# The Differential layer rebuilt: weights split one layer ahead, the convolution on VectorE alone and its inputs placed among the attention heads

## The chip, the cores and the metric

The kernel runs on one NeuronCore of a Trainium2 chip. The metric is the device time of one execution in microseconds (us); the median of three runs of the kernel before is 2931.03 us (2930.87 to 2932.01). Engines are named as in the profile: PE is TensorE (matmul), PEld its weight loads, DVE VectorE, ACT ScalarE, POOL GpSimd, SP the engine that issues the DMAs.

## The reference

Four mixer layers in a row (stages a0, b, c, a1), then two layers that each have a mixer and a SwiGLU feed-forward (m0, f0, m1, f1), on 512 tokens of width 1024 in float32. The change touches m0, the Differential layer, above all:

```python
def sandwich(x, g_pre, g_post, fn):
    return x + rmsnorm(fn(rmsnorm(x, g_pre)), g_post)

def even_mixer(t, ...):                     # m0
    proj = t @ w_in
    y_a = diff_attention(proj[..., :3 * DIFF_WIDTH], ...)
    y_b = conformer_conv(proj[..., 3 * DIFF_WIDTH:], dw_w, dw_b, ln_g, ln_b)
    return jnp.concatenate([y_a, y_b], axis=-1) @ w_out

def diff_attention(qkv, ...):               # 4 heads, two score maps each
    ...
        p = jax.nn.softmax(jnp.where(chunk_causal_mask(i, s), sc, -jnp.inf), axis=-1)
        w = p[:, :, 0] - lam * p[:, :, 1]
        return jnp.einsum('bhqk,bkhe->bqhe', w.astype(v.dtype), v)
    ...
    o = rmsnorm(o, subln) * (1.0 - lam_init)

def conformer_conv(g, dw_w, dw_b, ln_g, ln_b):   # 512 channels, 31 taps
    u = g[..., :CONV_CHANNELS] * jax.nn.sigmoid(g[..., CONV_CHANNELS:])
    y = lax.conv_general_dilated(u, dw_w[:, None, :], ..., feature_group_count=CONV_CHANNELS) + dw_b
    return jax.nn.silu(layernorm(y, ln_g, ln_b))
```

m1, the other mixer, is a state-space layer beside a latent attention; f0 and f1 are `(silu(h @ w_gate) * (h @ w_up)) @ w_down`.

## The kernel before

The activations x stay transposed on the chip: eight blocks of 128 features by 512 tokens. A float32 product is made of three matmuls in a reduced float32 form (fp32r). Every weight chunk of 128 x 1024 (512 KB) is loaded by SP into `wr`, copied by ACT into a high part `wh`, and the low part is `wl = wr - wh`, a subtraction on DVE; then the products wh·xh, wl·xh and wh·xl go into one PSUM sum. This is `wchunk`; `wr`, `wh` and `wl` have three buffers each. One chunk feeds 24 matmuls of 512 columns. `gemm_T` makes one output block from one chunk, `gemm_tok` a block of tokens from four.

In m0 every third chunk is split on POOL instead (`share`), in two halves (L284), and so are two of the four chunks with which the next layer begins (`wchunk(srcs[1], D, G)` in `sandwich_end`). m0 first makes all four convolution inputs (eight chunks `m0_wab`), then queries and keys of heads 0 and 1 (`project(0)`), the values, and `project(1)`. Of the 31 taps of a channel block 23 run on DVE as one multiply-add each (tile `cv`), 8 on ACT and POOL (L1091, L1092, tile `cvg`). Convolution and heads are generators in the list `tasks`; `tick` moves each of them on by one step between the matmuls of the other work. When all four convolution outputs are ready, `sandwich_end` multiplies by `m0_wo`, whose rows are ordered convolution first and heads 0 to 3 behind it, normalizes, adds to x, splits the new x (`xh`, `xl`) and starts the next layer's first panels by halves of the tokens.

A scheduler fixes each engine's order of instructions when the program is built, so every engine, and SP's DMA queue too, works through a list: an instruction that waits holds up what stands behind it. Nearly all DVE and PE instructions carry line L205, that of a helper, so they are told apart by their tiles: `g` and `a` are PSUM tiles, `x` the activations, `y` the inputs of an output product, `P` and `Ps` softmax rows, `mxc` a row maximum.

Of the kernel before, what the change touches and what calls it, by code (L numbers as in the profile page):

```python
# [4 lines left out]
P = 128  # L5
NT = 512
# [34 lines left out]
def prepare(inp):  # L41
# [75 lines left out]
    A["m0_wo"] = _panels(np.concatenate([w[512:], w[:512]], axis=0))  # L117
# [62 lines left out]
def build(nc, tc, A, out, stages=("a0", "b", "c", "a1", "m0", "f0", "m1", "f1")):  # L180
# [40 lines left out]
    with ctx:  # L221
# [49 lines left out]
        share = [0, 0]  # L271

        def wchunk(src, n, eng=None):
            if eng is None:
                share[1] += 1
                eng = G if share[0] and share[1] % share[0] == 0 else V
            wr = early.pop(0) if early else fetch(src, n)
# [550 lines left out]
        def layer_c(nxt):  # L828
            with ExitStack() as c:
                pp = newpool(c, "pcl")  # L830
                pp5 = newpool(c, "pcm", 5)
                X = state["X"]
                first, sc, sb = opening([A["c_wx"][i] for i in range(3)], X)
                csc = load(pp, "c_sc")
                ic = load(pp, "c_ic")
                pads = [tl(pp, (P, 16 + NT), f"pad{i}") for i in range(6)]
                for t in pads:
                    V.memset(t[:, 0:16], 0.0)
                npad = [0]

                def pad():
                    npad[0] += 1
                    return pads[npad[0] % 6]
                new_norm(nxt)
                for half in range(2):
                    Y = []
                    for g in (2 * half, 2 * half + 1):
                        wd = 2 << g
                        M = []
                        for i in range(4):  # L850
                            ps = first.pop(0) if first else gemm_T(A["c_wx"][g * 4 + i], X)
# [12 lines left out]
                            V.tensor_tensor(df[:, :16], fx, xc[:, 16:32], op=SUB)  # L864
                            M.append(split(pp5, "m", df))
                        Z = []
                        for i in range(4):
                            pz = gemm_T(A["c_wz"][g * 4 + i], X)
                            z = tl(pp, (P, NT), "z", bufs=5)
                            V.tensor_tensor(z, pz, sb, op=MUL)  # L870
                            S.activation(z, z, AF.Silu)
                            Z.append(z)
                        for i in range(4):
                            ps = gemm_T(A["c_wg"][g, i], M)
                            V.scalar_tensor_tensor(Z[i], ps, csc[:, g * 4 + i:g * 4 + i + 1], Z[i],
                                                   op0=MUL, op1=MUL)
                            Y.append(split(py, "y", Z[i]))
                    for m in range(KD):
                        ps = gemm_T(A["c_wo"][half, m], Y)
                        V.tensor_tensor(xs[m], xs[m], ps, op=ADD)  # L880
                        if half:
                            finish_x(m)()

        def ffn_first(l):
            return [A[f"f{l}_w{n}"][i] for i in range(2) for n in "gu"] if f"f{l}" in stages else None

        def m1_first():
            return [A["m1_win"][i] for i in (2, 0, 1, 3)] if "m1" in stages else None


        def sandwich_end(W, Y, O, fresh, grow, srcs, pre=None, k0=0):
# [82 lines left out]
            if srcs:  # L974
                W1 = wchunk(srcs[1], D, G)
# [13 lines left out]
            W2 = wchunk(srcs[2], D, G)  # L989
# [55 lines left out]
        def layer_m0(nxt):  # L1045
            with ExitStack() as c:
# [3 lines left out]
                first, sc, sb = opening([A["m0_wab"][i] for i in range(3)], X)  # L1050
# [23 lines left out]
                def conv(i, up, y):  # L1074
                    def w(k):
                        return dw[:, i * 31 + k:i * 31 + k + 1]

                    def u(k):
                        return up[:, 2 + k:2 + k + NT]
                    nv = 31 - CONV_G  # L1080
                    g = tl(pm, (P, NT), "cvg")
                    for k in range(nv):
                        if k == 0:
                            V.tensor_scalar(y, u(0), w(0), cb[:, i:i + 1], op0=MUL, op1=ADD)
                            S.activation(g, u(nv), AF.Copy, scale=w(nv))
                        else:
                            V.scalar_tensor_tensor(y, u(k), w(k), y, op0=MUL, op1=ADD)
                        q = nv + 1 + k // 3
                        if k % 3 == 2 and q < 31:
                            t = tmp()  # L1090
                            S.activation(t, u(q), AF.Copy, scale=w(q))  # L1091
                            G.tensor_tensor(g, g, t, op=ADD)  # L1092
                        if k % 4 == 4 - 1:
                            yield
                    V.tensor_tensor(y, y, g, op=ADD)

                def convs():
                    for i in range(4):
                        yield from conv(*CV[i])
                        if i == 1:  # L1100
                            total = tl(pm, (P, NT), "cb")
                        if i:
                            G.tensor_tensor(total, C[0] if i == 1 else total, C[i], op=ADD)
                    ps = psum_a()
                    PE.matmul(ps, lhsT=ones, rhs=total, start=True, stop=True)
# [3 lines left out]
                    ln = SumSq(4)  # L1109
                    for i in range(4):  # L1110
                        V.tensor_tensor(C[i], C[i], mu, op=SUB)
                        ln.add(C[i], i)
                    yield
                    r = small(4, "lnr")
                    rstd(r, ln.sums(), 1.0 / 512, 1e-5)
                    lb = bcast(diagonal(r), pm, "cb")
                    yield
                    for i in range(4):
# [5 lines left out]
                        Y[i] = split(py, "y", C[i], 0.5)  # L1124
                        yield
                CV = []
                for i in range(4):
                    pu = first.pop(0) if first else gemm_T(A["m0_wab"][2 * i], X)
                    pb = first.pop(0) if first else gemm_T(A["m0_wab"][2 * i + 1], X)
# [10 lines left out]
                    if i == 0:  # L1140
                        tasks.append(convs())


                def project(a):

                    pss = gemm_tok([A["m0_wqk"][a, i] for i in range(4)], X, NT, 2)
# [27 lines left out]
                def attend(h, T):  # L1174
# [40 lines left out]
                    Y[4 + h] = split(py, "y", ps, sub)  # L1215
                share[:] = [3, 0]
                q = project(0)
                T = [flip_qk(q, 0), flip_qk(q, 1)]
                pss = gemm_tok([A["m0_wv"][i] for i in range(4)], X, NT, 2)
# [4 lines left out]
                tasks.append(attend(1, T[1]))  # L1224
                q = project(1)
# [6 lines left out]
                sandwich_end(A["m0_wo"], Y, [tl(pa, (P, NT), "qkT") for _ in range(KD)], True, 8, ffn_first(0), k0=4)  # L1232


# [132 lines left out]
        def layer_m1(nxt):  # L1367
            with ExitStack() as c:
# [91 lines left out]
                def glu():  # L1460
# [4 lines left out]
                    wh, wl = wchunk(A["s_wg"], 512)  # L1465
# [27 lines left out]
                for i in range(2):  # L1493
                    ps = gemm_T(A["m1_win"][4 + i], X)
# [7 lines left out]
                wh, wl = wchunk(A["m1_wk"], 768)  # L1502
# [10 lines left out]
                wh, wl = wchunk(A["m1_wv"], 768)  # L1513
# [11 lines left out]
                for a in range(3):  # L1525
                    wh, wl = wchunk(A["m1_wq"][a], 1024)
# [53 lines left out]
                sandwich_end(A["m1_wo"], Y, O + [tl(pm, (P, NT), f"u{i}") for i in range(2)], True, 10, ffn_first(1))  # L1580


        def layer_f(l, nxt):
            with ExitStack() as c:
# [31 lines left out]
        pdr0 = newpool(ctx, "pdr0", space=bass.MemoryType.DRAM)  # L1616
# [42 lines left out]
```

## Time and profile before

| | |
|---|---|
| median of 3 runs | 2931.03 us |
| profiled execution, its own time | 2936.18 us |
| its span | 2933.7 us |
| mean granted TensorE clock | 0.976 |
| busy: PE, DVE, ACT, POOL | 96%, 56%, 36%, 12% |
| bytes moved | 270 MB, mean 92 GB/s |

The span is from the first to the last instruction; the execution's own time lies 2.5 us above it. In the trace m0 is at about 1643 to 1958 us, f0 at 1958 to 2250, m1 at 2250 to 2570, layer c at 973 to 1277. In a window row each engine has its busy time in that stretch and its instructions in brackets; PEclk is the granted clock as a share of full speed.

### The profile page before, as it was taken

The numbers are of one execution on the slowest core, as the hardware profiler recorded it, in microseconds if no ns is written. First come the engines' busy times: TensorE is split into PE (matmuls) and PEld (weight loads), VectorE is DVE, ScalarE is ACT, GpSimd is POOL, SyncE is SP. The second block draws the span as 40 slices with busy tenths as digits, with TensorE's granted clock in tenths as the row PEclk, the third lists the DMA queues.
The fourth block names the chain that finished last, engine by engine and source line by source line (L and its number), as shares of the span: only waits on it lengthen the run. The fifth ranks groups of instructions, "written<-read, shape, count | busy, mean of one in ns | idle before, by whom it ended". The sixth has DMA issues, their size and how long they took to land. (4 is left out here: it accounts for less than half of the span.)

```text
span 2933.7 us, 34524 instructions
## 1 busy us (share of the span) xinstructions
PE 2820.6 (96%) x13488; PEld 2331.9 (79%) x13488; DVE 1642.2 (56%) x3023; ACT 1051.9 (36%) x1679; POOL 347.3 (12%) x272
## 2 busy tenths in 40 slices
PE   8999999999999999999999987889999979999998
PEld 7888888888888888888888865678888845888886
DVE  4454654545556554544445697896443696543434
ACT  4322344444444322333223445442222435432222
POOL 2000000000000111210010252120000341300001
PEclk9999999999999999999999997889999999999999
DMA  4222332222223232322222211123332320132222
GB/s 161 94 86 94 129 111 87 87 80 94 72 94 95 94 101 89 120 93 94 93 94 92 90 63 44 48 96 136 111 105 92 113 90 22 58 101 100 94 99 67
DMA packets 87667, 270.08 MB, mean 92 GB/s; under 512 B 11728, under 2 KB 18640, under 8 KB 87504
## 3 DMA queue, kind: packets, MB, share of 16 engines
q1 hardware_dynamic: 87504, 267.88, 27.6%
q8 instruction: 105, 1.72, 0.2%
q14 instruction: 58, 0.48, 0.1%
HBM read 255.26 MB, written 12.58 MB: 91 GB/s over the span
## 5 line engine op out<-in xcount | busy, mean ns | idle before, releaser
L280 ACT ACTIVATE wh<-wr 128x1024 fp32r<-128x1024 f32 (+2 forms) x464 | 479.9, 1035 | 1329.8 <-PE g L205 1015.7
L205 DVE TENSOR_TENSOR wl<-wr,wh 128x1024 fp32r<-128x1024 f32 (+2 forms) x454 | 566.3, 1248 | 341.3 <-ACT wh L280 338.7
L205 PE MATMUL g<-xl,wh 128*128 128x512 f32 (+1 forms) x1720 | 661.6, 385 | 17.2 <-DVE xl L205 17.0
L205 PE MATMUL g<-xh,wh 128*128 128x512 f32 (+1 forms) x1720 | 663.7, 386 | 0.7 <-ACT wh L280 0.7
L205 PE MATMUL g<-xh,wl 128*128 128x512 f32 (+1 forms) x1720 | 658.1, 383 | 0.8 <-DVE wl L205 0.8
L205 PE MATMUL g<-wh,xh 128*128 128x512 f32 (+1 forms) x992 | 383.1, 386 | 16.9 <-ACT wh L280 8.9
L205 PE MATMUL g<-yh,wh 128*128 128x512 f32 (+1 forms) x1046 | 394.9, 378 | 1.4 <-DVE qr L205 1.4
L205 PE MATMUL g<-yh,wl 128*128 128x512 f32 (+1 forms) x1046 | 391.4, 374 | 3.1 <-DVE wl L205 3.1
L205 PEld LDWEIGHTS g<-xl,wh 128*128 128x128 f32 x1720 | 327.1, 190 | 83.0 <-DVE xl L205 22.9
L205 PE MATMUL g<-yl,wh 128*128 128x512 f32 (+1 forms) x1046 | 391.2, 374 | 0.0
L205 PE MATMUL g<-wl,xh 128*128 128x512 f32 (+1 forms) x992 | 377.8, 381 | 0.5 <-DVE wl L205 0.5
L205 PEld LDWEIGHTS g<-xh,wl 128*128 128x128 f32 x1720 | 327.3, 190 | 63.2 <-DVE wl L205 1.4
L205 PE MATMUL g<-wh,xl 128*128 128x512 f32 (+1 forms) x992 | 376.6, 380 | 0.0
L205 PEld LDWEIGHTS g<-xh,wh 128*128 128x128 f32 x1720 | 327.5, 190 | 61.2 <-ACT wh L280 1.2
L424 POOL TENSOR_TENSOR acc<-acc,t 128x256 f32<-128x256 f32 (+1 forms) x111 | 129.8, 1170 | 1654.5 <-issue 1406.4
L205 PEld LDWEIGHTS g<-wh,xh 128*128 128x128 f32 x992 | 188.5, 190 | 50.4 <-ACT wh L280 8.9
L205 PEld LDWEIGHTS g<-yh,wh 128*128 128x128 f32 x1046 | 198.4, 190 | 37.9 <-DVE qr L205 1.8
L205 PEld LDWEIGHTS g<-yh,wl 128*128 128x128 f32 x1046 | 198.1, 189 | 38.1 <-DVE wl L205 4.2
L205 PEld LDWEIGHTS g<-yl,wh 128*128 128x128 f32 x1046 | 198.3, 190 | 35.4 <-issue 1.2
L205 DVE TENSOR_TENSOR t<-g,sb 128x512 f32<-128x512 f32 x112 | 77.2, 690 | 251.4 <-PE g L205 251.4
L205 PEld LDWEIGHTS g<-wh,xl 128*128 128x128 f32 x992 | 188.4, 190 | 34.7 <-issue 0.2
L205 PEld LDWEIGHTS g<-wl,xh 128*128 128x128 f32 x992 | 188.6, 190 | 33.9 <-DVE wl L205 1.6
(315 smaller groups left out, 2728.5 us busy)
## 6 DMA issues: line engine op xcount, KB each, us to landing
wr<-in_f_wg_dram SPq DMA_DIRECT2D x44, 512.0 KB, 3.5
wr<-in_f_wu_dram SPq DMA_DIRECT2D x44, 512.0 KB, 3.5
wr<-in_a_wv_dram SPq DMA_DIRECT2D x32, 512.0 KB, 3.5
wr<-in_a_wu_dram SPq DMA_DIRECT2D x32, 512.0 KB, 3.4
wr<-in_a_wz_dram SPq DMA_DIRECT2D x32, 512.0 KB, 3.4
wr<-in_a_wo_dram SPq DMA_DIRECT2D x32, 512.0 KB, 3.5
wr<-in_b_wc_dram SPq DMA_DIRECT2D x32, 512.0 KB, 3.5
wr<-in_f_wd_dram SPq DMA_DIRECT2D x32, 512.0 KB, 3.5
```

Source lines behind the costliest of these rows:

```text
L205: r = f(*a, **k)
L280: S.activation(wh[:, :n], wr[:, :n], AF.Copy)
L424: G.tensor_tensor(self.acc[:, t], self.acc[:, t], sq[:, t], op=ADD)
```

## The change

1. A class `Pre` stands for a weight chunk that is split ahead of its layer. The task `presplit` loads it (`pr`, one buffer), lets ACT make `ph` and DVE `pl`, and stores both to DRAM. 32 chunks (m0's 28 and the first four of f0) are split while layer c runs, 24 chunks (m1's 20 and the first four of f1) while f0 runs. In m0, m1 and at the two seams behind them `wchunk` then loads `wh` and `wl` from there, 512 KB each, and no engine computes.
2. All splits, all 31 taps and the sums of the convolution's layer norm leave POOL. The taps are on DVE, the sums are matmuls with a tile of ones.
3. `conv_in(0)` and `conv_in(1)` come first, `conv_in(2)` behind the values, `conv_in(3)` behind `project(1)`.
4. The rows of `m0_wo` are ordered heads 0 and 1, convolution, heads 2 and 3; the kernel enters `sandwich_end` when the outputs of heads 0 and 1 are there.
5. Layer c finishes its tasks before its last output product, and the tables of the state-space layer are queued behind `presplit` in f0.

```diff
-    A["m0_wo"] = _panels(np.concatenate([w[512:], w[:512]], axis=0))
+    A["m0_wo"] = _panels(np.concatenate([w[:256], w[512:], w[256:512]], axis=0))
...
+        def presplit(pool, todo):
+            made = []
+
+            def store():
+                w, wh, wl = made.pop(0)
+                nc.sync.dma_start(w.h, f32(wh))
+                nc.sync.dma_start(w.l, f32(wl))
+            for w in todo:
+                n = w.n
+                wr = tl(pool, (P, 1024), "pr")[:, :n]
+                wh, wl = (tl(pool, (P, 1024), "p" + a, F32R, bufs=2)[:, :n] for a in "hl")
+                nc.sync.dma_start(wr, w.src)
+                if made:
+                    store()
+                yield
+                S.activation(wh, wr, AF.Copy)
+                V.tensor_tensor(wl, wr, f32(wh), op=SUB)
+                made.append((w, wh, wl))
+            store()
+
+        def wchunk(src, n):
             wh = tl(pw, (P, 1024), "wh", F32R)
             wl = tl(pw, (P, 1024), "wl", F32R)
+            if isinstance(src, Pre):
+                nc.sync.dma_start(f32(wh[:, :n]), src.h)
+                nc.sync.dma_start(f32(wl[:, :n]), src.l)
+                return wh, wl
+            wr = early.pop(0) if early else fetch(src, n)
             S.activation(wh[:, :n], wr[:, :n], AF.Copy)
-            step = n if eng is V else 512
-            for o in range(0, n, step):
-                e = slice(o, o + step)
-                eng.tensor_tensor(wl[:, e], wr[:, e], f32(wh[:, e]), op=SUB)
+            V.tensor_tensor(wl[:, :n], wr[:, :n], f32(wh[:, :n]), op=SUB)
...
+                if "m0" in stages:
+                    tasks.append(presplit(newpool(c, "pre"), m0_weights() + (ffn_first(0) or [])))
...
+                    if half:
+                        drain()
...
-                W1 = wchunk(srcs[1], D, G)
+                W1 = wchunk(srcs[1], D)
...
-                    nv = 31 - CONV_G
-                    g = tl(pm, (P, NT), "cvg")
-                    for k in range(nv):
+                    for k in range(31):
+                        u, w = up[:, 2 + k:2 + k + NT], dw[:, i * 31 + k:i * 31 + k + 1]
                         if k == 0:
...
-                            S.activation(g, u(nv), AF.Copy, scale=w(nv))
...
-                            G.tensor_tensor(g, g, t, op=ADD)
-                        if k % 4 == 4 - 1:
+                        if k % 5 == 5 - 1:
                             yield
-                    V.tensor_tensor(y, y, g, op=ADD)
...
-                PE.matmul(ps, lhsT=ones, rhs=total, start=True, stop=True)
+                for i in range(4):
+                    PE.matmul(ps, lhsT=ones, rhs=C[i], start=i == 0, stop=i == 3)
...
+                conv_in(0)
+                tasks.append(convs())
+                conv_in(1)
...
+                conv_in(2)
                 q = project(1)
...
-                share[0] = 0
-                while any(Y[k] is None for k in range(4)):
+                conv_in(3)
+                while any(Y[k] is None for k in range(2)):
                     tick()
-                sandwich_end(A["m0_wo"], Y, [...], True, 8, ffn_first(0), k0=4)
+                sandwich_end([pre("m0_wo", m) for m in range(KD)], Y, [...], True, 8, ffn_first(0), k0=2)
...
+                            tasks.append(presplit(newpool(c, "pre"), m1_weights() + (ffn_first(1) or [])))
                             tasks.append(ssm_tables(ptab))
```

The order of two engines is shown at two places. First SP's DMA queue in the output product of layer c, before (`wr` is the raw chunk of the layer itself):

```order
L254 DMA wr_8595<-in_c_wo_dram 128x1024
L254 DMA wr_8627<-in_c_wo_dram 128x1024
L254 DMA wr_8659<-in_c_wo_dram 128x1024
L254 DMA wr_8691<-in_c_wo_dram 128x1024
L254 DMA wr_8723<-in_c_wo_dram 128x1024
```

and at the same place after the change (`pr` is the raw chunk of m0, `preh` and `prel` the stores of its two parts):

```order
L286 DMA preh_1503_7921<-ph_8860 128x1024
L292 DMA pr_8899<-in_m_wo_dram 128x1024
L287 DMA prel_1504_7922<-pl_8861 128x1024
L254 DMA wr_9028<-in_c_wo_dram 128x1024
L286 DMA preh_1506_7923<-ph_8900 128x1024
L292 DMA pr_8939<-in_m_wo_dram 128x1024
L287 DMA prel_1507_7924<-pl_8901 128x1024
L254 DMA wr_9068<-in_c_wo_dram 128x1024
```

Each load of layer c now stands behind one load, and two stores, of a chunk that is split ahead; the load of `pr` waits until DVE has done with the chunk before it.

Second, DVE in m0, where the convolution ends, before (`cv` a multiply-add of the last channel block, `d` and `Ps` head pieces; the next `cv` row, the sum with `cvg`, stands 60 rows further down):

```order
L205 RECIPROCAL d_2408_13276<-d_2408_13276 128x2
L205 TENSOR_TENSOR wl_14043<-wr_14040,wh_14042 128x1024
L205 TENSOR_TENSOR d_2408_13276<-d_2408_13276,nl_12580 128x1
L205 SCALAR_TENSOR_TENSOR cv_2327_12822<-up_2326_12819,m_dw_12571,cv_2327_12822 128x512
L205 SCALAR_TENSOR_TENSOR Ps_13279<-Ps_13279,d_2408_13276,Ps_13285 128x128
L205 SCALAR_TENSOR_TENSOR cv_2327_12822<-up_2326_12819,m_dw_12571,cv_2327_12822 128x512
L205 ISA Ps_13394,mxc_13395<-a_13392,cmask_12592 128x256
```

and after the change, at the convolution's last taps:

```order
L205 TENSOR_REDUCE ssq_2759_14176<-t_14178 128x4
L205 SCALAR_TENSOR_TENSOR cv_2667_13888<-up_2666_13885,m_dw_12889,cv_2667_13888 128x512
L205 TENSOR_SCALAR rq_2760_14177<-ssq_2759_14176 128x4
L205 SCALAR_TENSOR_TENSOR yl_14202<-a_14196,m_sub_12903,yh_14201 128x512
L205 SCALAR_TENSOR_TENSOR cv_2667_13888<-up_2666_13885,m_dw_12889,cv_2667_13888 128x512
L205 TENSOR_TENSOR t_14183<-g_13935,rq_2760_14177 128x512
L205 SCALAR_TENSOR_TENSOR cv_2667_13888<-up_2666_13885,m_dw_12889,cv_2667_13888 128x512
L205 TENSOR_TENSOR cv_2480_12921<-cv_2480_12921,t_14194 128x512
L205 SCALAR_TENSOR_TENSOR yl_14211<-a_14205,m_sub_12903,yh_14210 128x512
L205 TENSOR_TENSOR cv_2486_12963<-cv_2486_12963,t_14194 128x512
L205 TENSOR_TENSOR cv_2555_13420<-cv_2555_13420,t_14194 128x512
L205 TENSOR_TENSOR cv_2667_13888<-cv_2667_13888,t_14194 128x512
```

No weight split stands there any more, and the layer norm (`cv` less its mean in `t`) follows right behind the last tap, which itself stands behind the last softmax rows of heads 2 and 3.

## Rows read from the trace of the kernel before

**Rows 1.** The page: its first line and TensorE's busy time (us, share, instructions).
```profile
span 2933.7 us, 34524 instructions
...
PE 2820.6 (96%) x13488; PEld 2331.9 (79%) x13488; DVE 1642.2 (56%) x3023; ACT 1051.9 (36%) x1679; POOL 347.3 (12%) x272
```

**Rows 2.** Windows of layer c and of FFN 0; columns in the first line.
```profile
core 0: us, PE busy (x) PEld busy (x) DVE busy (x) ACT busy (x) POOL busy (x), PEclk, DMA share, GB/s
975.00:1050.00 75.00, 75.00 (x341) 62.32 (x340) 45.08 (x76) 25.68 (x33) 6.76 (x4) 1.00 0.27 88
1950.00:2025.00 75.00, 75.00 (x341) 62.20 (x340) 65.49 (x229) 26.74 (x36) 1.02 (x1) 1.00 0.44 150
2025.00:2100.00 75.00, 75.00 (x334) 61.97 (x333) 29.21 (x45) 17.35 (x23) 0.00 (x0) 1.00 0.33 109
```

**Rows 3.** Windows of the Differential layer, columns as in Rows 2.
```profile
1650.00:1725.00 75.00, 62.94 (x279) 51.57 (x277) 65.81 (x80) 28.71 (x41) 28.05 (x17) 0.95 0.24 79
1725.00:1800.00 75.00, 60.91 (x263) 47.14 (x263) 67.80 (x119) 33.97 (x67) 30.06 (x19) 0.86 0.16 57
1800.00:1875.00 75.00, 61.80 (x245) 43.38 (x242) 50.62 (x171) 42.28 (x101) 14.52 (x12) 0.73 0.04 11
1690.00:1770.00 80.00, 55.77 (x236) 44.68 (x234) 79.65 (x95) 29.58 (x45) 40.80 (x24) 0.87 0.19 63
```

**Rows 4.** Timeline, TensorE: start, us, engine, line, operation, tiles, [idle before <-releaser].
```profile
1770.83 0.79 PE L205 MATMUL a<-qkT,qkT 64*128 64x128 f32 x2 [10.82 <-DVE mxc L205]
...
1898.42 0.39 PE L205 MATMUL g<-yh,wl 128*128 128x256 f32 x1 [2.84 <-DVE wl L205]
...
2416.53 0.80 PE L205 MATMUL a<-xl,xh 128*128 128x128 f32 x2 [9.92 <-DVE t L205]
```

**Rows 5.** Groups of instructions, 1645 to 1960: busy us, mean ns | idle before.
```profile
L205 DVE SCALAR_TENSOR_TENSOR cv<-up,m_dw,cv 128x512 f32<-128x512 f32 x88 | 85.8, 1020 | 0.1
...
L1092 POOL TENSOR_TENSOR cvg<-cvg,t 128x512 f32<-128x512 f32 x28 | 45.4, 1622 | 63.5 <-ACT t L1091 50.1 <-ACT cvg L1085 12.4
...
L205 DVE TENSOR_TENSOR wl<-wr,wh 128x1024 fp32r<-128x1024 f32 x27 | 36.6, 1362 | 10.7 <-ACT wh L280 10.7
...
L284 POOL TENSOR_TENSOR wl<-wr,wh 128x512 fp32r<-128x512 f32 x12 | 18.5, 1564 | 15.7 <-ACT wh L280 15.7
```

**Rows 6.** Groups of instructions, 2025 to 2100 (all splits of one shape).
```profile
L205 DVE TENSOR_TENSOR wl<-wr,wh 128x1024 fp32r<-128x1024 f32 x14 | 17.2, 1226 | 2.3 <-ACT wh L280 2.3
...
L280 ACT ACTIVATE wh<-wr 128x1024 fp32r<-128x1024 f32 x14 | 14.9, 1061 | 58.0 <-PE g L205 42.6 <-issue 15.4
```

**Rows 7.** DMA issues: the page; 2318 to 2350 (count, KB, us to landing).
```profile
wr<-in_f_wd_dram SPq DMA_DIRECT2D x32, 512.0 KB, 3.5
...
wr<-in_m_wq_dram SPq DMA_DIRECT2D x3, 512.0 KB, 4.7
```

**Rows 8.** Windows of layer m1 and of the end of FFN 0, columns as in Rows 2.
```profile
2335.00:2340.00 5.00, 5.00 (x31) 4.43 (x31) 2.38 (x9) 2.62 (x4) 1.02 (x1) 1.00 1.04 415
2410.00:2420.00 10.00, 3.47 (x8) 2.00 (x8) 10.00 (x16) 2.71 (x4) 6.68 (x5) 0.50 0.19 52
2225.00:2250.00 25.00, 25.00 (x112) 20.68 (x111) 10.70 (x12) 7.95 (x10) 0.00 (x0) 1.00 0.26 83
```

**Rows 9.** Timeline, VectorE: convolution taps and the last split of the Differential layer.
```profile
1767.84 2.73 DVE L205 SCALAR_TENSOR_TENSOR cv<-up,m_dw,cv 128x512 f32<-128x512 f32 x4
...
1866.23 1.40 DVE L205 SCALAR_TENSOR_TENSOR yl<-a,m_sub,yh 128x512 fp32r<-128x512 f32 x2
```

**Rows 10.** Timeline, TensorE: a last projection matmul and a first output one.
```profile
1792.82 0.40 PE L205 MATMUL g<-wh,xl 128*128 128x512 f32 x1
...
1864.79 0.48 PE L205 MATMUL g<-yh,wh 128*128 128x512 f32 x1
```

**Rows 11.** Groups of instructions, 2360 to 2400.
```profile
L205 DVE TENSOR_TENSOR wl<-wr,wh 128x1024 fp32r<-128x1024 f32 (+1 forms) x5 | 6.6, 1341 | 0.0
```

**Rows 12.** Groups of instructions, 2530 to 2620.
```profile
L205 PE MATMUL g<-xl,wh 128*128 128x512 f32 (+1 forms) x119 | 43.2, 363 | 5.5 <-DVE xl L205 5.4
```

More of the change, by code (lines that the diff above doesn't have):

```diff
@@ L882, in layer_c, with pre, m0_weights, m1_weights @@
                             finish_x(m)()
+        PRE = {}
+        def pre(name, *ix):
+            k = (name,) + ix
+            if k not in PRE:
+                a = A[name]
+                for i in ix:
+                    a = a[i]
+                PRE[k] = Pre(a, a.shape[-1])
+            return PRE[k]
         def ffn_first(l):
-            return [A[f"f{l}_w{n}"][i] for i in range(2) for n in "gu"] if f"f{l}" in stages else None
+            return [pre(f"f{l}_w{n}", i) for i in range(2) for n in "gu"] if f"f{l}" in stages else None
         def m1_first():
-            return [A["m1_win"][i] for i in (2, 0, 1, 3)] if "m1" in stages else None
+            return [pre("m1_win", i) for i in (2, 0, 1, 3)] if "m1" in stages else None
+        def m0_weights():
+            return ([pre("m0_wab", i) for i in range(8)] + [pre("m0_wqk", a, i) for a in range(2) for i in range(4)]
+                    + [pre("m0_wv", i) for i in range(4)] + [pre("m0_wo", m) for m in range(KD)])
+        def m1_weights():
+            return (m1_first() + [pre("m1_win", i) for i in (4, 5)] + [pre("m1_wk"), pre("m1_wv")]
+                    + [pre("m1_wq", a) for a in range(3)] + [pre("s_wg")] + [pre("m1_wo", m) for m in range(KD)])
         def sandwich_end(W, Y, O, fresh, grow, srcs, pre=None, k0=0):
@@ L988, in sandwich_end @@
                 return
-            W2 = wchunk(srcs[2], D, G)
+            W2 = wchunk(srcs[2], D)
             X = state["X"]
@@ L1049, in layer_m0 @@
                 X = state["X"]
-                first, sc, sb = opening([A["m0_wab"][i] for i in range(3)], X)
+                first, sc, sb = opening([pre("m0_wab", i) for i in range(3)], X)
                 new_norm(nxt)
@@ L1108, in convs @@
                     yield
-                    ln = SumSq(4)
+                    sqs = []
                     for i in range(4):
                         V.tensor_tensor(C[i], C[i], mu, op=SUB)
-                        ln.add(C[i], i)
+                        sq = tmp()
+                        S.activation(sq, C[i], AF.Square)
+                        sqs.append(sq)
                     yield
                     r = small(4, "lnr")
-                    rstd(r, ln.sums(), 1.0 / 512, 1e-5)
+                    ps = psum_a()
+                    for n in range(4):
+                        for i in range(4):
+                            PE.matmul(ps[:, n:n + 1], lhsT=sqs[i][:, n * P:(n + 1) * P], rhs=ones[:, 0:1],
+                                      start=i == 0, stop=i == 3)
+                    rstd(r, ps[:, 0:4], 1.0 / 512, 1e-5)
                     lb = bcast(diagonal(r), pm, "cb")
@@ L1123, in convs, with conv_in @@
                         V.scalar_tensor_tensor(C[i], t, 1.0, C[i], op0=ADD, op1=MUL)
-                        Y[i] = split(py, "y", C[i], 0.5)
+                        Y[2 + i] = split(py, "y", C[i], 0.5)
                         yield
                 CV = []
-                for i in range(4):
-                    pu = first.pop(0) if first else gemm_T(A["m0_wab"][2 * i], X)
-                    pb = first.pop(0) if first else gemm_T(A["m0_wab"][2 * i + 1], X)
+                def conv_in(i):
+                    pu = first.pop(0) if first else gemm_T(pre("m0_wab", 2 * i), X)
+                    pb = first.pop(0) if first else gemm_T(pre("m0_wab", 2 * i + 1), X)
                     b = tmp()
@@ L1214, in attend @@
                         PE.transpose(ps[:, i * P:(i + 1) * P], o[:, i * P:(i + 1) * P], ident)
-                    Y[4 + h] = split(py, "y", ps, sub)
-                share[:] = [3, 0]
+                    Y[h if h < 2 else 4 + h] = split(py, "y", ps, sub)
                 q = project(0)
                 T = [flip_qk(q, 0), flip_qk(q, 1)]
-                pss = gemm_tok([A["m0_wv"][i] for i in range(4)], X, NT, 2)
+                pss = gemm_tok([pre("m0_wv", i) for i in range(4)], X, NT, 2)
                 vt = tl(pm, (P, 4, NT), "vt")
```

49 lines of the change are left out of this document (18 added, 31 removed).

## The prediction

> **What bounds the kernel now.** I read the page first: TensorE is busy for 96% of the span [rows 1], so only the 113 us in which it is not can be won, apart from slow clock. The windows say where those lie. In layer c and in FFN 0 TensorE is busy for all of each 75 us at full clock [rows 2]; nothing can be gained there, only lost. In m0 the three windows from 1650 to 1875 hold 185.7 us of TensorE in 225, with clocks of 0.95, 0.86 and 0.73, and from 1690 to 1770 TensorE is idle for 24.2 us of 80 while VectorE is busy for 79.65 [rows 3]: there m0 is bound by VectorE. The timeline names the waits: 10.82 us on a softmax row maximum, that stood on VectorE behind convolution taps and splits, 2.84 on a split in the output product, and in m1 9.92 us on VectorE [rows 4]. The change takes work from VectorE at those places and puts it into the two layers where TensorE has no idle time.
>
> **Cost in layer c and FFN 0.** 32 chunks go into c, 24 into f0, each with one ACT copy of 1.06 us and one VectorE subtraction of 1.23 [rows 6] and 1.5 MB of DMA. Engine time is there: c's window has 45.08 of 75 us on VectorE, and some 12 more splits make about 60; f0's first window has 65.49 and would overflow by about 5, which the free 46 of the next one take [rows 2], since the tables of the state-space layer are queued behind the splits. What can bind is the chain. `pr` has one buffer, so one chunk takes load, copy, subtraction one after the other: 3.5 us to landing [rows 7], 1.06, a hand-over of 2.3/14 = 0.16, and 1.23 [rows 6], 5.95 us in all. And it is coupled to TensorE, since each raw load of the layer itself stands on SP behind a `pr` load that waits for VectorE. In c 25 splits stand beside 24 whole and 8 half chunks of the layer: 28 x 24 matmuls at 75/334 = 0.2246 us [rows 2] are 151 us, 6.04 us for each split. In f0 24 stand beside 27 chunks, 146 us, 6.08 each. So the bare chain just fits. Nearest rows for a loaded queue: a load of the same size took 4.7 us where the DMA was busy in m1 [rows 7]. I take 3.9, a third of the way, since the order issues the `pr` load ahead of the low part's store and the layer's load, and 0.3 for queueing on VectorE, in order behind a subtraction of 1.23: 6.65 us. Buffers (three raw, three split) let TensorE run ahead; I take two chunks, 11 us, once in each layer. Loss: 25 x 0.61 - 11 = 4 in c, 24 x 0.57 - 11 = 3 in f0, **7 us**; bounds 0 (bare chain) and 46 (below).
>
> The bytes also limit. In c 25 x 1.57 + 28 x 0.524 = 54 MB in 151 us are 357 GB/s. The row nearest to a full queue has 415 GB/s at a share of 1.04 [rows 8], so the engines would be 86% busy; scaled from c's own window (88 GB/s at 0.27, so 326 when full, [rows 2]) they would need 166 us, 15 more. Both are inside the bounds. The Trainium skill ("DMA: Bandwidth & Descriptors", Specifications) gives about 358 GB/s from HBM for one core; by that c needs all of its 151 us and every gap in the chain would be paid. The row of 415 GB/s contradicts it, and the sum goes by the row.
>
> **Gain in m0's body.** Of VectorE's work in 1645 to 1960 the 27 splits leave, 36.6 us. The 88 taps took 1020 ns on the mean beside POOL [rows 5], and four of them 2.73, 0.68 each, where POOL rests [rows 9]; 120 and the four first ones at 0.7 make 87 us for 85.8, so 32 more taps cost nothing once POOL's 45.4 and 18.5 us [rows 5] are gone. So much of the 24.2 us in 1690 to 1770 should go. But the end of the body moves too. Both orders have 20 chunks of 24 matmuls up to the last projection; it ends at 1793 now [rows 10]. Afterwards the last chunk is that of `conv_in(3)`, behind both `project`s and behind the heads' turning and most of heads 0 and 1, which now come after; that puts back what the waits gave, and I get 1796. Then VectorE still has all the taps of block 3 (30 x 0.68 = 20 us) and the softmax, layer norm and split work of heads 2 and 3 and the convolution, some 34 us by durations in this stretch; all in order. About 10 us more are chained waits: mean, squares, their sum, root, spread, each crossing PE, ACT and VectorE. That gives 1860 for the last split, against 1866.2 [rows 9]. The output matmuls left at that point are about as many as now (174 of 192, against some 177 behind 1864.8 [rows 10]). Gain **6 us**; bounds -6 (if `conv_in(3)` ends 12 us later) and 39, all idle time of 1650 to 1875 [rows 3]. I stay near the low end, because the convolution's last block is now late by construction of the order.
>
> **The seams and m1.** At m0's end the wait of 2.84 for a split [rows 4] goes, and one split of 1.23 ahead of the updates: **4 us**. At the end of f0 TensorE is never idle, 25.00 of 25 [rows 8], so the split there is hidden today and the gain is **0**. At the end of m1 TensorE waits 5.4 us on `xl` [rows 12]; POOL's halves slow those, and I take half, **3 us**. In m1 VectorE runs without a gap before the wait of 9.92, at 10.00 of 10 [rows 8]; the five splits in 2360 to 2400 are 6.6 us [rows 11] and all stand ahead of the late instruction. What is late next are POOL and DMA results. Against it, m1's first loads double in bytes just where the queue is full (415 GB/s): two chunks of 384 KB and two of 512, 1.8 MB, 4 us later, of which a part shows. **5 us**, bounds 0 and 10. The clock granted after that wait is 0.50 [rows 8]; if it stays up there is a little more, not counted.
>
> **The sum.** 6 + 4 + 0 + 3 + 5 - 7 = 11 us less. From the profiled execution's 2936.2 that gives 2925.2; it ran 5.2 us above the median of the runs, so I predict **2920 us**. Taps, copies and subtractions in c and f0 cost nothing beyond the chain because TensorE's matmuls cover them. If that cover is gone, they cost what the first rival says.
>
> **Rivals.**
> - *The chain of splits starves TensorE in c and f0* (slower). One buffer, a load that waits on VectorE, and the layer's own loads behind it on SP. With loads of 4.7 us, as measured in the busy stretch of m1 [rows 7], and the same 0.3, a chunk takes 7.45: 25 x 1.41 - 11 = 24 and 24 x 1.37 - 11 = 22, 46 us of loss, and -18 + 46 = +28, **2959 us**. It decides against the change from 6.9 us a chunk on, where the loss eats all 18. For it: 357 GB/s on 415. Against it: the loads stand first in each round, and today's layers take 3.5 with a queue at 0.27 to 0.44 [rows 2].
> - *m0 becomes bound by TensorE* (much faster). If VectorE, free of splits and of POOL, keeps ahead all through, the 39 us of idle time in 1650 to 1875 go rather than 6: 33 more, **2887 us**. For it: VectorE at 79.65 of 80 is the bound now. Against it: heads and layer norm are chains, and TensorE stood 13 us idle in 1800 to 1875 with VectorE at 50.62 of 75 [rows 3].
> - *The late convolution eats the rest* (no change). If `conv_in(3)` ends at 1808, since heads 0 and 1 are now ahead of it, the last split is at 1872, m0 loses 6 in place of winning 6, and the sum is about 0: **2931 us**.
>
> **Chances and range.** Forecast 0.50, starved chain 0.25, TensorE-bound m0 0.13, late convolution 0.12. The forecast's own range is 2906 to 2932: m0's and m1's bounds without their far ends, and 0 to 20 for c and f0. The range of 2890 to 2956 leaves out about 0.08 below and 0.12 above. A measurement of this kernel can tell about 0.2%, 6 us: faster by more is the TensorE-bound case and most of the forecast, 0.59; within it 0.15; slower by more, 0.26, the starved chain and a little beside it.
>
> **What would show it.** Right: layer c and f0 with TensorE at 75 of 75, or with gaps of a few us put down to the DMA of `wr` or `wl`; `pr` landing under 4 us; taps at 0.68 to 0.74; no gap of 10.82 in m0 but a gap on the layer norm just before the output product, and the last split near 1860 on today's clock; m1's wait of 9.92 down to about 3. Wrong: gaps of over 10 us in c or f0, a clock below 1.00 there, `pr` landing above 4.5; or m0 with hardly a gap; or the last split of m0 later than today's.

## The result, and the profile after

The changed kernel takes 2952.23 us (median of 4 runs, 2948.16 to 2957.14), the one before 2930.95 beside it: a ratio of 1.0075, 95% interval 1.0058 to 1.0093. It is slower by 21 us where 11 us less was forecast; the first rival, splits that starve TensorE, gave 2959.

Where the time went is read by putting the same event of both traces side by side: a table of starts (us), from the timelines of VectorE and TensorE.

| event | before | after | difference |
|---|---|---|---|
| first product scaled in layer c (`z<-g,sb`) | 999.78 | 1010.42 | +10.6 |
| first sums of layer a1 (`a<-t,ones`) | 1302.62 | 1338.38 | +35.8 |
| last update of x at m0's end (`x<-x,qkT`) | 1942.57 | 1958.37 | +15.8 |
| last update of x at f0's end (`x<-x,o`) | 2325.92 | 2349.76 | +23.8 |
| last update of x at m1's end (`x<-x,u`) | 2564.23 | 2581.20 | +17.0 |
| end of the span | 2933.7 | 2950.4 | +16.7 |

So c and the seam ahead of it lost 35.8 us, m0 won 20.0, f0 with its end lost 8.0, m1 with its end won 6.9. The kernel before was profiled in an execution 5.2 us above its median (2936.18 against 2931.03), the changed one at its median (2952.30 against 2952.23), so the table ends at +16.7 where the medians differ by 21.3. The traces that split nothing in c agree with the kernel before up to a1 within 4 us, two of them within 0.2, and from m1's end to the span's end all three traces that were compared (before, change, run 3) take 369.2 to 369.5 us; so the wins from m0 to m1 can be up to 5 us too large against a median execution.

The windows of c after the change, columns as in [rows 2] (length, then TensorE, its loads, VectorE, ACT, POOL, the granted clock, DMA share, GB/s):

```profile
975.00:1050.00 75.00, 69.57 (x304) 57.53 (x303) 47.92 (x70) 31.86 (x39) 4.60 (x4) 0.95 0.74 255
1050.00:1125.00 75.00, 69.09 (x285) 54.85 (x284) 44.73 (x61) 29.87 (x36) 4.82 (x3) 0.95 0.85 292
1125.00:1200.00 75.00, 67.22 (x271) 51.92 (x270) 42.38 (x53) 25.16 (x28) 10.95 (x8) 0.95 0.80 279
```

Before, each of these windows had 75.00 of 75 and a clock of 1.00 (the first is in [rows 2]). Here 19.1 us of 225 are idle, and the clock of 0.95 takes some 11 more, an estimate (0.05 of 225): the waits cost more than half their length again in clock.

The chain of the splits is seen on VectorE, here its `pl` rows in the output product of c, and on SP, the DMAs of one of the rounds (start, us, engine, line, operation, tiles, idle before and its releaser):

```profile
1107.73 1.23 DVE L205 TENSOR_TENSOR pl<-pr,ph 128x1024 fp32r<-128x1024 f32 x1 [0.99 <-ACT ph L296]
...
1129.07 1.23 DVE L205 TENSOR_TENSOR pl<-pr,ph 128x1024 fp32r<-128x1024 f32 x1 [2.94 <-ACT ph L296]
1135.90 1.23 DVE L205 TENSOR_TENSOR pl<-pr,ph 128x1024 fp32r<-128x1024 f32 x1 [3.12 <-ACT ph L296]
1142.74 1.23 DVE L205 TENSOR_TENSOR pl<-pr,ph 128x1024 fp32r<-128x1024 f32 x1 [3.04 <-ACT ph L296]
```

```profile
1107.73 0.33 SPq L286 DMA_DIRECT2D preh<-ph  x1
1108.99 0.33 SPq L292 DMA_DIRECT2D pr<-in_m_wo_dram  x1
1109.37 0.44 SPq L287 DMA_DIRECT2D prel<-pl  x1
1109.86 0.42 SPq L254 DMA_DIRECT2D wr<-in_c_wo_dram  x1
...
1116.03 0.33 SPq L292 DMA_DIRECT2D pr<-in_m_wo_dram  x1
```

A `pl` ends at 1108.96, and at 1108.99 SP issues the next raw load; only then can it issue the layer's own load of `wr`. One round takes 6.84 us here, 7.30 on the mean of the 24 rounds from 1012.24 to 1187.39, beside 5.4 us of TensorE's work for one chunk. On VectorE each of the later `pl` shown waits 3 us for ACT's copy, which waits for the DMA; all that is queued behind it waits too. In 975 to 1200 these are 54.8 us in 24 waits.

SP is held up as well. Its longest wait in 975 to 1200, before and then after the change (us in total, times, longest):

```profile
SPq L254 <- DVE wl L205: 204.0, 46, 9.8
```

```profile
SPq L286 <- ACT ph L296: 104.0, 26, 5.5
```

Before, SP waited only for free buffers of the layer's own chunks, so it ran ahead of TensorE as far as they allow. Now it waits 104.0 us for ACT's copy before it can issue the store `preh`, with the layer's own loads behind it; ACT waits 14.2 us for loads of `wr` in this stretch, and did not wait for them before. DMA issues of 975 to 1200 (count, KB, median us to landing):

```profile
preh<-ph SPq DMA_DIRECT2D x28, 512.0 KB, 2.8
prel<-pl SPq DMA_DIRECT2D x28, 512.0 KB, 5.4
wr<-in_c_wz_dram SPq DMA_DIRECT2D x11, 512.0 KB, 6.1
pr<-in_m_wqk_dram SPq DMA_DIRECT2D x8, 512.0 KB, 4.9
pr<-in_m_wo_dram SPq DMA_DIRECT2D x8, 512.0 KB, 4.5
```

Loads of this size landed in 3.5 us before [rows 7], those of `in_m_wqk` and `in_m_wo` in m0 (1640 to 1960) too. At the seam ahead of c seven chunks are split before c's first scale is made; TensorE then waits for VectorE:

```profile
995.03 2.08 PE L205 MATMUL a<-t,ones 128*128 128x128 f32 x8 [5.43 <-DVE t L205]
```

In m0 the gaps of [rows 4] are gone. The last matmul of the last projection and the layer norm chain behind it, TensorE's timeline after:

```profile
1816.43 0.39 PE L205 MATMUL g<-xh,wl 128*128 128x512 f32 x1
...
1868.02 0.58 PE L205 MATMUL a<-ones,t 128*128 128x1 f32 x2 [1.86 <-ACT t L1148]
1869.29 6.91 PE L205 MATMUL a<-ones,t 128*128 128x1 f32 x30 [0.68 <-ACT t L1148]
1877.86 2.07 PE L205 MATMUL a<-t,ones 128*128 128x128 f32 x8 [1.66 <-DVE t L205]
1884.72 1.22 PE L205 MATMUL g<-yh,wh 128*128 128x512 f32 x2 [4.79 <-ACT yh L421]
```

and VectorE's last tap and last split of the convolution, with the group of the taps (count, busy, mean ns):

```profile
1863.19 0.74 DVE L205 SCALAR_TENSOR_TENSOR cv<-up,m_dw,cv 128x512 f32<-128x512 f32 x1
...
1890.21 0.69 DVE L205 SCALAR_TENSOR_TENSOR yl<-cv,yh 128x512 fp32r<-128x512 f32 x1 [0.70 <-ACT yh L421]
```

```profile
L205 DVE SCALAR_TENSOR_TENSOR cv<-up,m_dw,cv 128x512 f32<-128x512 f32 x120 | 87.1, 751 | 1.4
```

m0 started 35.7 us late (its opening, the last `x<-x,t` of a1, stands at 1680.05 against 1644.33). These taken off, the last matmul of the projections stands at 1780.7, 12 us earlier than in [rows 10], and the last split at 1854.5 against 1866.2 in [rows 9]. From the last tap to the last split are 27 us, in which no more taps are left to fill the waits. In m1 the wait of 9.92 us of [rows 4] is there unchanged, to the hundredth:

```profile
2436.27 0.80 PE L205 MATMUL a<-xl,xh 128*128 128x128 f32 x2 [9.92 <-DVE t L205]
```

### The profile page after: what moved, and what is told of

Read it like the earlier page. It is cut to its first block, busy times and chain, and to the rows that moved or that the text cites. A ratio compares the mean times of both kernels' runs of the same rounds, so it can differ in the third digit from the quotient of the medians.

```text
span 2950.4 us, 34843 instructions
## 1 busy us (share of the span) xinstructions
PE 2829.6 (96%) x13510; PEld 2328.2 (79%) x13510; DVE 1630.0 (55%) x3061; ACT 1034.1 (35%) x1647; POOL 256.3 (9%) x219
## 5 line engine op out<-in xcount | busy, mean ns | idle before, releaser
L309 ACT ACTIVATE wh<-wr 128x1024 fp32r<-128x1024 f32 (+2 forms) x408 | 420.8, 1033 | 1029.5 <-PE g L205 792.2
L205 DVE TENSOR_TENSOR wl<-wr,wh 128x1024 fp32r<-128x1024 f32 (+2 forms) x408 | 508.2, 1246 | 308.8 <-ACT wh L309 305.9
L205 PE MATMUL g<-yh,wh 128*128 128x512 f32 (+1 forms) x1046 | 398.3, 381 | 10.6 <-ACT yh L421 4.8
L450 POOL TENSOR_TENSOR acc<-acc,t 128x256 f32<-128x256 f32 (+1 forms) x109 | 121.8, 1118 | 1671.1 <-issue 1412.9
```

What stands on the lines that cost most here:

```text
L205: r = f(*a, **k)
L450: G.tensor_tensor(self.acc[:, t], self.acc[:, t], sq[:, t], op=ADD)
```

## The experiments

Times beside each run are its own median and its ratio to the kernel before on the same chip. The segments of each, as in the table above (difference to before, us; c with the seam up to a1's first sums, then up to the last update of x of m0, f0 and m1; the column of m0 holds a1 too):

| run | c | m0 | f0 | m1 |
|---|---|---|---|---|
| the change | +35.8 | -20.0 | +8.0 | -6.9 |
| 1 no split in c | +2.3 | -15.1 | +11.7 | -4.0 |
| 2 no split in f0 | +40.1 | -18.7 | -3.0 | -2.1 |
| 3 no split ahead | +1.0 | -15.2 | -3.3 | -1.7 |
| 4 paced | +12.2 | -18.7 | -0.8 | -6.1 |
| 5 f0 alone, paced | +0.8 | -15.7 | -1.0 | -7.4 |
| 6 no stores | +8.5 | -16.7 | +1.1 | -1.7 |
| 7 paced, two raw buffers | +5.5 | -18.8 | -0.3 | -5.5 |
| 8 taps on POOL again | -0.1 | -13.4 | -3.3 | -1.6 |
| 9 split in a1 | +0.7 | -17.2 | +1.1 | -6.0 |
| 10 rows as before | 0.0 | -8.2 | -3.3 | -1.6 |
| 11 inputs as before | +3.8 | -29.2 | -3.4 | -1.8 |
| 12 inputs first, f0 paced | +0.4 | -31.8 | 0.0 | -5.6 |

Each segment is from one profiled execution, which can lie some 5 us off its kernel's median (run 11's is 5.1 above, run 12's 3.8 below). Runs 1, 3, 5 and 8 to 12 split nothing in layer c and differ there by up to 4 us, so less than that is not read as a difference.

**Which layer costs it (runs 1 to 3).** The edit of run 1 (run 2 does the same for m1 and f1 in f0, run 3 both):

```diff
-                PRE[k] = Pre(a, a.shape[-1])
+                PRE[k] = a if name in ('m0_wab', 'm0_wqk', 'm0_wv', 'm0_wo', 'f0_wg', 'f0_wu') else Pre(a, a.shape[-1])
...
-                if "m0" in stages:
-                    tasks.append(presplit(newpool(c, "pre"), m0_weights() + (ffn_first(0) or [])))
```

> The 32 chunks of m0 and f0 are split in m0 again (on VectorE), nothing is split in layer c; all else as after the change. Theory A (splitting ahead starves TensorE in c): the +35.8 us between the first kernel and the changed one at the start of layer a1 goes to within 2 us of zero; m0 gives back 8 to 16 of the 19.9 us it won, so about 2952 - 36 + 12 = 2928 us. Theory B (c is slower because its tasks are drained before its last output product, or because instructions moved): c stays 20 us or more slower, total 2955 to 2965.

Run 1: 2931.15 us, ratio 1.0005 (0.9996 to 1.0015). c's loss goes down to 2.3 us, though the tasks are still drained before its last output product: theory B falls. m0 gives back 5 us, not the 8 to 16 expected.

> The 24 chunks of m1 and f1 are split in place, nothing is split in f0; c as after the change. Theory A: the 8 us that f0 with its end loses go, the 7 us that m1 with its end won go too: 2951 us, within 5, c unchanged at +35.8. Theory B: as A here, since it speaks of c alone. If m1's 7 us came from other parts of the change, 2944.

Run 2: 2950.69 us, ratio 1.0074 (1.0051 to 1.0097), as expected in sum. f0 turns from a loss of 8.0 into a win of 3.0; m1 gives back 4.7 of its 6.9.

> No chunk is split ahead, all are split on VectorE in their own layer; the convolution on VectorE alone, its inputs among the heads and the reordered output rows stay. Theory A: the sum of the two runs before it, 2952 - 36 + 12 - 8 + 7 = 2927 us, c and f0 at 75 of 75 in their windows. Theory B: 2950 or above.

Run 3: 2915.79 us, ratio 0.9954 (0.9937 to 0.9972). Without any split ahead, the rest of the change is faster by some 13 us, and 11 below the 2927 expected, since m0 gives back less than that sum has and f0 wins 3.3 in place of losing nothing; the only edit left in f0 is that POOL splits nothing at its end. Splits ahead are worth 3.5 to 5 us in m0 (runs 2 and 3, the change and run 1) and 2 to 5 in m1, and cost 34 to 39 in c and 11 to 15 in f0.

**What about the splits costs it (runs 4, 6 and 7).** Run 4 gives each chunk two steps and keeps VectorE's part in its place of the program:

```diff
                 yield
                 S.activation(wh, wr, AF.Copy)
+                old, pinned[0] = pinned[0], (V,)
                 V.tensor_tensor(wl, wr, f32(wh), op=SUB)
+                pinned[0] = old
                 made.append((w, wh, wl))
+                yield
```

> Splits ahead as after the change, but one chunk for two chunks of the layer, and VectorE's split kept in its place of the program, so that the 32 chunks spread over all of c (304 us of matmuls, 9.5 us a chunk) and the 24 over all of f0. Theory A with the chain as cause (7.3 us a chunk, 5.4 to 6 us of TensorE work beside it): with 9.5 us of work beside each the chain fits, c loses under 8 us, f0 under 3: 2952 - 28 - 6 = 2918 us. If instead every byte or every split costs TensorE time wherever it stands, c still loses 25 to 36 and the time is 2945 to 2952.

Run 4: 2922.40 us, ratio 0.9978 (0.9967 to 0.9989). The same bytes and splits, spread over all of c, cost 12.2 us for 35.8, over all of f0 about 2.5 (-0.8 against -3.3 without any). So neither the bytes nor the number of the splits costs the 35.8 us by itself. The run changes two things at once, the pace and VectorE's place in the order, and does not part them. It was expected that c loses under 8 us; most of the 12.2 sits in one window, which has 73.48 us of TensorE at 1.00 in the kernel before:

```profile
1200.00:1275.00 75.00, 68.56 (x282) 54.38 (x281) 43.48 (x57) 29.36 (x38) 15.75 (x11) 0.95 0.68 229
```

Run 6 stores nothing, and m0 and m1 load and split the raw chunks:

```diff
-                w, wh, wl = made.pop(0)
-                nc.sync.dma_start(w.h, f32(wh))
-                nc.sync.dma_start(w.l, f32(wl))
+                made.pop(0)
...
             if isinstance(src, Pre):
-                nc.sync.dma_start(f32(wh[:, :n]), src.h)
-                nc.sync.dma_start(f32(wl[:, :n]), src.l)
-                return wh, wl
+                src = src.src
```

> As after the change, but the split parts are not stored, and m0 and m1 load the raw chunk and split it in place: in c the loads and the splits stay, 1 of the 1.5 MB that a chunk moves goes. Theory A1 (traffic lengthens the load, the serial chain does the rest): pr lands in 3.5 to 3.8 us, a chunk takes 6.0 to 6.4 us, a1 starts 5 to 14 us later than in the first kernel in place of 35.8. Theory A2 (the waits of ph and pl in ACT's and VectorE's lists cost it, whatever the DMA does): a1 still starts 25 us or more later.

Run 6: one execution, 2926.54 us. Its DMA row of 975 to 1200 and two `pl` rows on VectorE:

```profile
pr<-in_m_wo_dram SPq DMA_DIRECT2D x8, 512.0 KB, 3.5
```

```profile
1127.83 1.23 DVE L205 TENSOR_TENSOR pl<-pr,ph 128x1024 fp32r<-128x1024 f32 x1 [2.89 <-ACT ph L294]
1133.75 1.23 DVE L205 TENSOR_TENSOR pl<-pr,ph 128x1024 fp32r<-128x1024 f32 x1 [2.97 <-ACT ph L294]
```

The load is back at 3.5 us, the round at 5.92 here, near the bare chain's 5.95 of the forecast, and at 6.37 on the mean of the 23 rounds from 1006.88 to 1153.42. c loses 8.5 us, 5.3 of them ahead of its first product. Its order was built anew, with the splits a little closer together. Theory A2 falls, since `pl` waits for `ph` as long as after the change (53.0 us in 975 to 1200, beside 54.8) and yet most of the loss is gone: some 27 of the 35.8 us go with the stores. The run does not part the two ways in which they act: they lengthen the loads, and SP waited 104.0 us for `ph` to issue them, a wait that is gone here.

Run 7 is run 4 with a second raw buffer (`pr` with bufs=2; `ph` gives one up, as the layer has no more room):

> The paced run with two raw buffers (and one for the high part), so that the next chunk loads while one is split; bytes and VectorE's order as in the paced run. Theory chain (one buffer: load, copy, split and next load are one chain): the 12.2 us that c lost in the paced run fall to under 5, 2915 us. Theory bytes (the queue is too full for the layer's own loads): c still loses 10 to 14, 2922 us.

Run 7: 2916.09 us, ratio 0.9948 (0.9927 to 0.9968). c's loss falls from 12.2 to 5.5 us, between both expectations, nearer to the chain's. The window that held run 4's loss:

```profile
1200.00:1275.00 75.00, 71.73 (x307) 58.32 (x306) 51.80 (x65) 35.92 (x47) 15.58 (x11) 0.98 0.76 266
```

It has more bytes per second than in run 4 and half of the idle time (3.3 us for 6.4), so there about half of the loss came of the single buffer and not of the bytes.

**Where m0's gain is from (runs 8, 10 and 11, each against run 3).** Run 8 puts 8 of 31 taps back on ACT and POOL, with the first kernel's `conv`.

> The run without any split ahead (2915.8), but 8 of 31 taps on ACT and POOL again as in the first kernel; inputs among the heads and the row order stay. If the order of the inputs and rows gave m0 its 15.1 us, m0 keeps 10 or more: 2916 to 2921. If the taps' return to VectorE alone gave it (0.75 us each now for 1.02 beside POOL), m0 keeps under 5: 2926 or above.

Run 8: 2917.28 us, ratio 0.9954 (0.9937 to 0.9970). m0 keeps 13.4 of 15.2: where the taps run hardly counts. Run 10 puts the output rows back into the first order (the indices of `Y` and `k0`, left out here, follow it):

```diff
-    A["m0_wo"] = _panels(np.concatenate([w[:256], w[512:], w[256:512]], axis=0))
+    A["m0_wo"] = _panels(np.concatenate([w[512:], w[:512]], axis=0))
...
-                while any(Y[k] is None for k in range(2)):
+                while any(Y[k] is None for k in range(4)):
...
```

> The run without any split ahead (2915.8), but with the output rows in the first kernel's order (convolution first) and the entry to the end part when the convolution's outputs are there. m0 won 15.1 us there. If the row order gives it, m0 keeps under 5 (2926 or above); if the place of the inputs gives it, over 10 (2915 to 2921).

Run 10: 2921.09 us, ratio 0.9968 (0.9955 to 0.9981). m0 keeps 8.2: the row order, with the entry that goes with it, is worth 7 us by the traces and 5 by the medians of runs 3 and 10. The 8.2 that are left are not the row order's, and up to 5 of them may be the 5.2 us by which the trace of the kernel before lies above its median. Run 11 makes all four convolution inputs first again, as in the first kernel:

```diff
                 conv_in(0)
                 tasks.append(convs())
-                conv_in(1)
+                for i in range(1, 4):
+                    conv_in(i)
...
-                conv_in(2)
                 q = project(1)
...
-                conv_in(3)
```

> The run without any split ahead, but all four convolution inputs first, as in the first kernel; the new row order stays. If the place of the inputs gives m0 its 15.1 us, m0 keeps under 5 (2926 or above); if the row order gives it, over 10 (2915 to 2921).

Run 11: 2899.56 us, ratio 0.9889 (0.9872 to 0.9906). Neither case foresaw it: m0 does not only keep its 15.2 but nearly doubles it, to 29.2. The place among the heads costs 14 us by the traces, 16 by the medians of runs 3 and 11. TensorE's timeline at the same place as above:

```profile
1830.88 2.08 PE L205 MATMUL a<-t,ones 128*128 128x128 f32 x8 [3.31 <-DVE t L205]
1839.15 1.22 PE L205 MATMUL g<-yh,wh 128*128 128x512 f32 x2 [4.48 <-ACT yh L421]
```

Counted from m0's opening, the first output product of the convolution starts 191.0 us on (1839.15 less 1648.13), against 204.7 after the change (1884.72 less 1680.05) and 207.7 in run 3 (1852.98 less 1645.26). VectorE's last tap stands 165.1 us on (1813.19), after the change 183.1.

**Versions that keep what helps (runs 5, 9 and 12).** Run 5 is run 1 with the paced splits in f0; run 9 splits m0's chunks in a1 with one chunk for two, in the layer's own raw buffers; run 12 is run 5 with the inputs first.

> No split ahead in c; in f0 the 24 chunks of m1 and f1 paced as in the paced run (one per two chunks of f0, VectorE's split kept in its place). From the segments of the runs so far: c +1, m0 -15.1 as without any split ahead, f0 -0.8 and m1 -6.1 as in the paced run: 2915.8 + 2.5 - 4.4 = 2914 us. If the f0 splits still cost what they cost unpaced (15 us beside an undisturbed c), 2926.

Run 5: 2912.70 us, ratio 0.9941 (0.9923 to 0.9959), near the 2914 expected.

> m0's and f0's 32 chunks split during layer a1 (366 us of matmuls, one for two chunks, 11 us each) in place of c, m1's in f0, both paced; the raw chunks share the layer's own three buffers, the parts have one buffer each. If pace is all that counts, c and a1 lose under 3 us together, m0 wins 18.6 and the rest is as in the run paced in f0 alone: 2912.7 - 3.6 + 2 = 2911 us. If a shared raw buffer takes away what the layer runs ahead, a1 loses 5 to 15: 2915 to 2925.

Run 9: 2911.40 us, ratio 0.9932 (0.9917 to 0.9947). Paced splits can be free: with 32 of them a1 takes 341.9 us from its first sums to its last update of x, against 341.7 in the kernel before. The run is not apart from run 5 by the intervals.

> All four convolution inputs first, as in the first kernel, with the new row order and the taps on VectorE; nothing split ahead in c; m1's and f1's chunks split in f0, one for two chunks. If the two gains add up (m0 -29 as in the run with the inputs first, f0 and m1 2 to 5 us better as in the run paced in f0 alone): 2899.6 - 3 = 2896 us. If the paced splits in f0 only pay for themselves: 2899 to 2901.

Run 12: 2902.51 us, ratio 0.9891 (0.9870 to 0.9912): the same as run 11 within the intervals, so whether the paced splits in f0 add anything is not shown. Runs 11 and 12 beat both kernels; run 11, with no split ahead at all, is the simpler one.

## Why the prediction was wrong, step by step

**The step that failed is the loss in c and f0**, taken as 4 and 3 us. c lost 35.8, f0 11 to 15 (its own end won 3). The mechanism was named, as the first rival; the forecast had its size wrong, in three places.
- *The round.* 6.65 us were taken, a third of the way from an idle queue to a busy one; 7.30 were measured, nearly the rival's 7.45. With 7.30 the forecast's own formula gives 25 x 1.26 - 11 = 20.5 us, against 25.2 from c's first product on. The landing was 4.5 to 4.9 in place of 3.9, and run 6 shows that the two stores do that: without them the load lands in 3.5 and the mean round is 6.37. The forecast took 3.9 because the load stands ahead of the low part's store and of the layer's load. That is so, but the high part's store stands ahead of it, in the order that was shown too: SP issues `preh` at 1107.73 and the load at 1108.99, and `preh` takes 2.8 us to land. SP's wait of 104.0 us for that store was in no term.
- *The full rate of the DMA.* 415 GB/s came from a stretch of loads alone [rows 8]. Beside stores the full queue moves less: in the five stretches of 5 us from 975 to 1200 with a share of 0.95 or more it moves 297 to 380 GB/s, 321 on the mean. The other bound given, 326 scaled from [rows 2], was the better one. The figure of 358 that the Trainium skill has ("DMA: Bandwidth & Descriptors", Specifications), which I set aside for the row of 415, agrees with this stretch better than that row did: only one of the five, the one of 380, lies above it. A limit it is not here, as that one and the row of 415 show.
- *The seam.* 10.6 us were lost ahead of c's first product and had no term at all. The scheduler pulled seven splits forward, and VectorE, in order, waited 1.9 to 4.4 us on each of the last five with the layer's statistics behind. In run 4, where VectorE's splits keep their place and the chunks are paced, +1.1 us are left of it.

The slow clock was in no term either: c's three windows lost some 11 us beside their 19 idle ones. Most of f0's loss lies in its first 100 us, where the splits run (TensorE 47.51 and 46.85 of 50 each, clocks 0.97 and 0.93, DMA share 0.79 and 0.89):

```profile
1961.70:2011.70 50.00, 47.51 (x219) 39.52 (x218) 42.83 (x126) 21.84 (x28) 1.06 (x1) 0.97 0.79 272
2011.70:2061.70 50.00, 46.85 (x194) 37.81 (x194) 27.18 (x38) 19.02 (x24) 0.00 (x0) 0.93 0.89 306
```

The first rival's 2959 came near for the right mechanism, but partly by luck: it had 24 us for c and 22 for f0, where 35.8 and 11 to 15 were lost.

**m0's body** was forecast at 6 us and its end at 4; both together won 20.0, of which up to 5 may be the 5.2 us by which the trace of the kernel before lies above its median. The waits went further than thought: the projections end 12 us earlier, not 3 later, as VectorE no longer holds them up. That the convolution comes late was right, and runs 3 and 11 show its price, 14 us; but from the last projection to the last split it took 74 us (1816.43 to 1890.21), not the 64 of the forecast (1796 to 1860), and 27 of them lie behind the last tap. Of these the group of 30 small matmuls for the squares alone takes 6.91 us on TensorE, at a clock of 0.50 (1869 to 1877). So the last split came at 1854.5 for the 1860 forecast because a longer tail followed an earlier start: two errors that nearly cancel. That the taps cost nothing was right (87.1 us for the 87 of the forecast), and run 8 shows that they could have stayed on POOL. Where the 8.2 us come from that run 10 keeps was not separated.

**The end of f0** was given 0, from a window at 2225 to 2250 that lies ahead of it. It stands at 2297 to 2326, and there TensorE was far from busy, in a window of the kernel before that was not read:

```profile
2295.00:2325.00 30.00, 23.91 (x151) 21.91 (x149) 27.34 (x54) 15.12 (x35) 17.95 (x19) 0.83 0.17 54
```

Runs 2, 3, 8, 10 and 11, which split nothing in f0, win 3.0 to 3.4 there. The clock of the stretch that matches it is 0.89 in run 3; how far the missing POOL splits, the clock or those 5.2 us make up the 3 us was not separated.

**m1** was forecast at 5 us and its end at 3; 6.9 were won. The sum was nearly right, by luck, and the main reason wrong: the 9.92 us on VectorE did not move. The wait lies between `qr` and `t`, and on VectorE these two have the same row of products and scans between them in both kernels, without a split; taking splits away ahead of them moves both ends. It stands in run 12 too. What shrank are other waits of TensorE from f0's end to m1's: 2.8 us for `bc` in place of 5.3, 4.3 for `xl` in place of 6.2, 0.4 for `qr` in place of 2.8, with 1.8 newly for loads of the split parts. Why they shrank was not tested.

So of the sum, the wins of 18 us were 27 in the traces and the losses of 7 were 44, with the win at f0's end counted in them: the losses decide the sign.

## What to carry to other kernels

Work that is hidden beside a busy TensorE cost much at one pace and little at another: compare the round of its whole chain, with the loads lengthened by its own stores, with the work that stands beside one round, and spread it until it fits. Where engines and queues work through lists in order, a side task with one buffer makes its own waits those of the layer, and so does a store that stands ahead of the layer's loads and waits for the task. And a gap in the profile stays, as the 9.92 us of m1 did, when the work that is taken away stands ahead of both its ends.

## What the runs showed of the hardware

- Two stores of 512 KB beside each load lengthen the load of the same size from 3.5 us (run 6) to 4.5 and 4.9 (the two groups of eight loads in the change), at a mean DMA share of 0.74 to 0.85.
- The most that loads and stores together moved in a 75-us window of c was 292 GB/s at a share of 0.85; the five fullest stretches of 5 us in it (share 0.95 to 1.01) had 297 to 380 (two of them below); loads alone had 415 at 1.04 [rows 8].

```profile
1035.00:1040.00 5.00, 5.00 (x24) 4.14 (x23) 5.00 (x7) 2.38 (x4) 0.00 (x0) 1.00 0.97 380
1085.00:1090.00 5.00, 3.32 (x12) 2.09 (x12) 3.74 (x5) 2.46 (x4) 0.00 (x0) 0.93 1.01 300
```

- Short waits on TensorE cost clock too. In 1050 to 1125 of the change none is longer than 1.51 us, 5.9 in all, two of them here, and yet the granted clock of that window is 0.95, between the levels of 1.2 and 2.4 GHz; without waits [rows 2] it is 1.00, the upper one. All six waits lie in the three 10-us windows below, and these are the only ones of 1050 to 1120 with a clock under 1.00.

```profile
1097.82 0.50 PE L205 MATMUL g<-yh,wl 128*128 128x512 f32 x1 [1.46 <-DVE wl L205]
...
1103.93 0.50 PE L205 MATMUL g<-yh,wh 128*128 128x512 f32 x1 [1.51 <-ACT yh L418]
```

```profile
1080.00:1090.00 10.00, 8.32 (x34) 6.23 (x34) 5.38 (x8) 4.00 (x6) 0.00 (x0) 0.97 0.98 313
1090.00:1100.00 10.00, 8.12 (x29) 5.88 (x29) 5.86 (x7) 4.97 (x7) 0.00 (x0) 0.86 0.82 286
1100.00:1110.00 10.00, 7.64 (x26) 5.59 (x25) 6.39 (x8) 4.34 (x5) 0.00 (x0) 0.83 0.92 323
```
